# Where the ada rows of a macaron layer are summed: rates of the row queue, and an earlier stage for one vector

## The chip, the cores and the metric

The kernel runs on one core of one Trainium2 chip. A core has TensorE (matmuls; PE in the profile, PEld its weight loads), VectorE (DVE), ScalarE (ACT), GpSimd (POOL) and SyncE (SP, which here only issues transfers), and 16 DMA engines that bring data from HBM to on-chip memory. The metric is device time in microseconds, the median of several executions; lower is better.

## The reference

One layer on 256 tokens of width 2048, in fp32: a half-weighted SwiGLU feed-forward, a token mixer of eight attention heads and four mLSTM heads, and a second feed-forward, each between an adaptive modulation and a gated residual with a layer norm.

```python
ada = (silu(c) @ w_ada + b_ada)                      # [1, 9*2048], w_ada is 2048 x 18432
sh1, sc1, g1, sh2, sc2, g2, sh3, sc3, g3 = split(ada, 9)
h = swiglu(ln(x) * (1 + sc1) + sh1, ffn1_w_in, ffn1_w_out)
x = ln(ALPHA * x + 0.5 * (1 + g1) * h, ln1_g, ln1_b)
h = mixer(ln(x) * (1 + sc2) + sh2, ...)              # w_in, heads, w_out
x = ln(ALPHA * x + (1 + g2) * h, ln2_g, ln2_b)
h = swiglu(ln(x) * (1 + sc3) + sh3, ffn2_w_in, ffn2_w_out)
x = ln(ALPHA * x + 0.5 * (1 + g3) * h, ln3_g, ln3_b)
```

The nine vectors of `ada` are numbered 0 to 8 in the kernel: 0, 3 and 6 are shifts, 1, 4 and 7 scales, 2, 5 and 8 gates. Each needs 2048 x 2048 weights, read once for a single row of `c`. The inner width of the feed-forwards is 5632.

## The kernel before, in words

**Matmuls.** All large products are done in three parts with split operands (`mm3`, lines 419 to 421): an operand is cast to a shortened format on ScalarE (`hi`, line 155) and the remainder is taken on VectorE (`lo`, line 156). Weights come in by `load_w`: a raw tile of 1 MB (three buffers, SyncE issues the transfer, line 382), then two splits of 128 x 1024 into `hi` and `lo` (six buffers each). A raw buffer is free again when both of its `lo` have been taken. Unless told otherwise one such load is 24 matmuls of 512 columns, or 48 of 256.

**Stages.** First feed-forward's input columns (`first_in`, then `ffn_in`), its output projection (`out_proj` with the tag `f1`), a hand-ordered `boundary` (residual, layer norm, modulation), the mixer's projections with the heads woven between (`cols_1024`, `cols_form_b`, `form_a_four`; `step` is called once per load), the mixer's output projection (`out_proj`, tag `mx`), a second boundary, and the second feed-forward in the same manner (tag `f2`).

**The output projection.** `out_proj` goes through the 2048 output columns in three passes, of widths 1024, 512 and 512. In the first pass the hidden rows are also split (`h_rows`). For the first feed-forward a pass is 22, 11 and 11 loads. The additions into the residual (`add_up`, which multiplies by `gate`) of one pass are put into the list `late` and carried out a few steps at a time (`catch_up`) during the next pass. `lastg` is true in the last pass. In that pass the last four loads have no pump; for `f1` they call `ada.end_step()` instead. `finish1` first calls `need(6)` and then sets `ada.owed` to 0.

**The ada rows.** VectorE sums the products of `w_ada` with `silu(c)`: for each of 16 blocks of 128 rows, a transfer of 128 x 1024 numbers (512 KB, into `araw`, two buffers, line 189) and one operation `acc = raw * csil + acc` (line 170). Such a step is called a row here. Sixteen rows make a unit: half a gate (1024 columns; two units per gate), or a pair, 512 columns each of a shift and of its scale (four units per pair of vectors). A unit ends with a tail of five steps (`pair_tail`, `gate_tail`): splits, a sum over the partitions by TensorE (`bc`, line 183), and for pairs a product with the identity and a reduction (lines 200 to 204).

The class `AdaQueue` holds the units in a fixed order: gate 2, pairs 3 (four units), `pair(6, 0)`, `pair(6, 1)`, gate 5, `pair(6, 2)`, `pair(6, 3)`, gate 8. `pump(rate)` is called once per weight load: it does one step of a waiting tail, adds the rate to `owed`, and issues rows while `owed` is at least 1. Two things hold a unit back: its `stage`, when the queue's `stage` is still lower, and the accumulator. A unit without a place of its own uses the one tile `acc`, and waits until no tail of another such unit is open; the credit goes on growing meanwhile. `pair(6, 1)` is summed in the lower half of the tile `gate`, which the first feed-forward's residual reads in the first pass of its projection; the second half of gate 5 is summed in the upper half, which the second and third passes read. `need(n)` runs rows and tails until n units are done.

The rates are `R_F` and `R_IN` for the first feed-forward's input columns, `R_OUT` for its output projection, `R_MX` for the mixer up to its output projection, and `R_A`, `R_B` for the second feed-forward.

**Order on the engines.** Each engine executes its instructions in a fixed order. A planner makes that order ahead of the run, from the program's order, the buffers and its own estimates; `pinned()` keeps a row behind the latest weight split and the latest use of hidden rows, and the boundaries are ordered by hand.

Of the kernel before, what the change touches and what calls it, by code (L numbers as in the profile page):

```python
# [32 lines left out]
def layer_kernel(  # L33
# [35 lines left out]
    def mm_tile(name, four=False):  # L69
        turn[0] = 0 if four else turn[0] % 5 + 1  # L70
        if turn[0] == 5:
            return fifth_tile(name)
        return pm.tile([P, 512], F32, tag="mm", bufs=4, name=name)
# [205 lines left out]
    ada = AdaQueue()  # L279
# [98 lines left out]
    def load_w(src, nk, w, name, by_parts=False, behind=None, into=None):  # L378
        raw = wp.tile([P, nk, w], F32, tag="raw", bufs=3, name=f"raw_{name}")
        src = src.rearrange("(k p) n -> p k n", p=P)  # L380
        if not by_parts:
            SP.dma_start(raw, src)
        h = nk // 2 if nk * w <= 2048 else nk // 4
        for q in range(nk // h):
            if by_parts:
                SP.dma_start(raw[:, q * h:(q + 1) * h], src[:, q * h:(q + 1) * h])
            if into:
                hi, los = into[q]
                S.copy(hi, raw[:, q * h:(q + 1) * h, :])
                n = h // len(los)  # L390
                for i, lo in enumerate(los):
                    pin["w"] = V.tensor_tensor(out=lo, in0=raw[:, q * h + i * n:q * h + (i + 1) * n, :],
                                               in1=hi[:, i * n:(i + 1) * n, :].bitcast(F32), op=ALU.subtract).ins
                for kk in range(h):
                    yield q * h + kk, hi[:, kk, :], los[kk // n][:, kk % n, :]
                continue
            hi = wp.tile([P, h, w], F32R, tag="hi", bufs=6, name=f"hi_{name}{q}")
            lo = wp.tile([P, h, w], F32R, tag="lo", bufs=6, name=f"lo_{name}{q}")
            with ExitStack() as s:
                if behind:  # L400
                    s.enter_context(tc.issue_after(behind))
                pin["w"] = split(raw[:, q * h:(q + 1) * h, :], hi, lo).ins
            for kk in range(h):
                yield q * h + kk, hi[:, kk, :], lo[:, kk, :]
# [46 lines left out]
    def out_proj(w, rows, nk, tag, npump, finish, before=None, turned=False, spare=None, fine=None):  # L451
# [3 lines left out]
        late = []  # L455


        def catch_up(n):
            while n and late:
                if next(late[0], 0) == 0:  # L460
                    late.pop(0)
                else:
                    n -= 1
        for width in (1024, 512, 512):
# [4 lines left out]
                us = us[nu // 2:] + us[nu // 4:nu // 2] + us[:nu // 4]  # L469
            ps = {(a, b): mm_tile(f"o_{tag}{col}{a}{b}") for b in range(nb) for a in range(2)}  # L470
            lastg = col + width == D
            held = []

            def products(a, args, last=us[-1] * kn + kn - 1):
                ts_ = slice(a * P, (a + 1) * P)
                for k, hh, hl, hi, lo in args:
                    for b in range(nb):
                        mm3(ps[a, b], hh[:, ts_], hl[:, ts_], hi[:, b * 512:(b + 1) * 512],
                            lo[:, b * 512:(b + 1) * 512], k == us[0] * kn, k == last)
# [25 lines left out]
            def add_up(a, ps=ps, col=col, bs=range(nb), stats=True):  # L505
                for b in bs:
                    cs = slice(col + b * 512, col + (b + 1) * 512)
                    r = res[:, a, cs]
                    o = unwoven(ps[a, b])
                    V.tensor_tensor(out=o, in0=o, in1=halves(gate[:, cs]), op=ALU.mult)  # L510
                    yield
                    V.scalar_tensor_tensor(out=halves(r), in0=halves(r), scalar=ALPHA, in1=o,
                                           op0=ALU.mult, op1=ALU.add)
                    yield
                    if a and stats:
                        add_stats(cs)
                    elif stats:
                        V.bn_stats(st[0][:, col // 512 + b, :], r)
                    yield

            for i, u in enumerate(us):
                hs = []
                if before:
                    before(u * kn)
                into = spare() if spare and lastg and i == nu - nheld else None
                for k in range(u * kn, u * kn + kn, 2):
                    hs += rows(k)
                for kk, hi, lo in load_w(w[u * kn * P:(u + 1) * kn * P, col:col + width], kn, width,
                                         f"{tag}o{col}_{u}", into=into):
                    arg = (u * kn + kk, *hs[kk], hi, lo)  # L530
                    if lastg and i >= nu - nheld or not lastg and i == nu - 1:
                        held.append(arg)
                    else:
                        for a in range(2):
                            if a and lastg and fine is not None:
                                products(a, [arg], nk - nheld * kn - 1)
                            else:
                                products(a, [arg])
                if not lastg and i == nu - 1:

                    late += [add_up(a, bs=(b,)) for b in range(nb) for a in range(2)]
                    products(0, held)
                    catch_up(2)
                    products(1, held)
                else:
                    catch_up(2)
                if not lastg or i < nu - 4:
                    npump()
                elif tag == "f1":
                    ada.end_step()  # L550
# [209 lines left out]
    def entry_of(load, got, u0, u1):  # L760
        for u in range(u0, u1):
            got[u] = []
            for item in load(u):
                got[u].append(item)
                yield

    R_F, R_IN, R_OUT, R_MX, R_A, R_B = 1.25, 1.2, 1, 1.42, 1.05, .6
    NP = 2  # L770
    right = dict(side="right")
    def at(rate):
# [223 lines left out]
    low, high = (lambda: gate[:, :1024]), (lambda: gate[:, 1024:])  # L996
# [2 lines left out]
        ada.pair(3, j)  # L999
    ada.pair(6, 0)  # L1000
    ada.pair(6, 1, low, stage=1)
    ada.gate(5, 1.0, None, high, stage=1)
    ada.pair(6, 2)
    ada.pair(6, 3, low, stage=2)
    ada.gate(8, 0.5, high, None, stage=2)
    for j in range(4):
        fa = first_ada(j + 1) if j < 3 else load_mixer_smalls()
        for i in range(NS):
# [79 lines left out]

    hi_places("1")
    out_proj(ffn1_w_out[0], h_rows, KF, "f1", at(R_OUT), finish1, spare=lambda: dead_rows(ln1_g, ln1_b, "1"))  # L1090
    xp, npool = ent["xp"], ent["np"]
    xT = new_xT("mx")
    raws = [mo_raw(u) for u in range(3)]
    mow = {}
    fence, _, xs, ws = boundary(*ent["f"], ent["lgb"], 3, "1", xT, entry_of(mo_load, mow, 3, 6), KD, raws)
    ada.stage = 1
    lnp.release()
    ent["pools"].pop().release()

# [11 lines left out]
    mx = tc.alloc_tile_pool(name="mx", bufs=1, **right)  # L1111
# [401 lines left out]
    def before(k):  # L1513
        until([f"row{i}" for i in (k, k + 1)])
        if k == 2:
            need(10)
# [42 lines left out]
    def dead_heads():  # L1559
        hi = mx.tile([P, 2, 2, 512], F32R, tag="yF", name="yw")  # L1560
        lo = [mx.tile([P, 1, 512], F32R, tag="qk", bufs=4, name=f"yw{k}") for k in range(4)]
        return [(hi[:, q], lo[2 * q:2 * q + 2]) for q in range(2)]

    out_proj(w_out[0], y_rows, KD, "mx", step, finish2, before, True, dead_heads)
    xp, npool = ent["xp"], ent["np"]
    xT = new_xT("f2")
    raws = [gu_raw(u) for u in range(3)]
    guw = {}
    fence, mr2, xs, ws = boundary(*ent["f"], lgb, 6, "2", xT, entry_of(gu_load, guw, 3, 4), 8, raws)
    ada.stage = 2  # L1570
    lnp.release()


# [76 lines left out]
    def finish3(products, add_up, st):  # L1650
        to_out(products, add_up, st, ent["lgb"])

    out_proj(ffn2_w_out[0], h_rows, KF, "f2", at(R_B), finish3, spare=lambda: dead_rows(ln3_g, ln3_b, "3"),
             fine=fine)
    ent["dead"].release()
# [32 lines left out]
```

## Time and profile before

| | us |
|---|---|
| median of three executions | 1882.77 |
| lowest and highest | 1878.36, 1888.13 |
| the profiled execution | 1878.17 |
| its span, first to last instruction | 1876.2 |
| TensorE busy | 1838.5 (98%) |
| VectorE busy | 1429.2 (76%) |
| ScalarE busy | 900.5 (48%) |

The stages, from the span's start: input columns of the first feed-forward to 525, its output projection 525 to 756, boundary 756 to 794, the mixer's projections and heads 794 to about 1050, its output projection to about 1150, boundary to about 1176, the second feed-forward to the end. The granted TensorE clock was 0.996 of full speed over the span. An engine's idle time matters here only where TensorE waits for it.

### The profile page before, as it was taken

To read this page: it belongs to the slowest core of one execution; us is meant where nothing else is said; L and a number is where in the kernel's file an instruction comes from. 1 tells how busy PE (TensorE), PEld (TensorE's weight loads), DVE (VectorE), ACT (ScalarE), POOL (GpSimd) and SP (SyncE) were. 2 spreads that over 40 slices of the span, in tenths; PEclk is the share of its full clock that TensorE was granted. 3 is DMA by queue.
4 is the path that set the end of the run, shared out by engine and by line. 5 is a ranking of instruction groups with operands and counts; after the bars stand their busy time and mean duration, and the time that the engine had idled before them with its cause. 6 is when DMAs were issued, how large, how long until landed. Compare 5 with 4: busy or idle time off the path is not lost.

```text
span 1876.2 us, 32153 instructions
## 1 busy us (share of the span) xinstructions
PE 1838.5 (98%) x13161; PEld 1719.4 (92%) x13161; DVE 1429.2 (76%) x1771; ACT 900.5 (48%) x1272; POOL 62.2 (3%) x92
## 2 busy tenths in 40 slices
PE   7999999999999999999989999999999999999997
PEld 5999999999998888699989887999999999988887
DVE  6889989778788886878889888868876665564655
ACT  3554453434463433845566645565444444454441
POOL 1211200000000000100000000000000000000000
PEclk9999999999999999999999999999999999999999
DMA  9979968999898897499879893988778766566663
GB/s 365 383 267 320 325 228 277 322 330 331 275 321 293 310 324 289 142 307 329 297 265 323 311 322 131 343 291 271 253 251 265 260 223 195 191 204 203 205 204 146
DMA packets 283915, 510.90 MB, mean 272 GB/s; under 512 B 10834, under 2 KB 134386, under 8 KB 282744
## 3 DMA queue, kind: packets, MB, share of 16 engines
q1 hardware_dynamic: 275656, 477.90, 75.0%
q0 software_dynamic: 8112, 30.95, 4.8%
q8 instruction: 103, 1.69, 0.4%
q14 instruction: 44, 0.36, 0.1%
HBM read 506.71 MB, written 2.10 MB: 271 GB/s over the span
## 4 chain that ended last, share of the span: by engine, by line
PE 42%; DMA 7%; DVE 7%; issue 2%; ACT 1%; POOL 0%; DVEq 0%; ACTq 0%; POOLq 0%
DMA ar<-in_w_ada_dram 6%; PE gu_f L420 5%; PE gu_f L419 5%; PE gu_f L421 5%; PE o_f L420 4%; PE o_f L419 4%; PE o_f L421 4%; PE fh L419 2%; PE fh L420 2%; PE fh L421 2%; PE fs L420 2%; PE fs L421 2%; PE fs L419 1%; DVE acc L170 1%; PE ge L747 1%
## 5 line engine op out<-in xcount | busy, mean ns | idle before, releaser
L170 DVE SCALAR_TENSOR_TENSOR acc<-ar,csil,acc 128x1024 f32<-128x1024 f32 (+1 forms) x167 | 211.9, 1270 | 73.0 <-DMA ar<-in_w_ada_dram 72.1
L419 PE MATMUL s<-xhi_f,hi_s 128*128 128x256 f32 x768 | 212.9, 278 | 1.1 <-DVE hT L969 0.9
L421 PE MATMUL s<-xhi_f,lo_s 128*128 128x256 f32 x768 | 212.4, 277 | 0.8 <-DVE lo_s L156 0.7
L420 PE MATMUL s<-xlo_f,hi_s 128*128 128x256 f32 x768 | 212.5, 277 | 0.0
L421 PE MATMUL gu_f<-xhi_f,lo_f2i 128*128 128x256 f32 x768 | 211.6, 275 | 0.0
L420 PE MATMUL gu_f<-xlo_f,hi_f2i 128*128 128x256 f32 x768 | 211.5, 275 | 0.0
L419 PE MATMUL gu_f<-xhi_f,hi_f2i 128*128 128x256 f32 x768 | 211.5, 275 | 0.0
L156 DVE TENSOR_TENSOR lo_f2i<-raw_f2i,hi_f2i 128x1024 fp32r<-128x1024 f32 x96 | 117.6, 1225 | 90.2 <-ACT hi_f2i L155 89.9
L421 PE MATMUL gu_f<-xhi_f,lo_f1i 128*128 128x256 f32 x640 | 176.5, 276 | 0.8 <-DVE lo_f1i L156 0.8
L420 PE MATMUL gu_f<-xlo_f,hi_f1i 128*128 128x256 f32 x640 | 176.3, 275 | 0.0
L419 PE MATMUL gu_f<-xhi_f,hi_f1i 128*128 128x256 f32 x640 | 176.3, 275 | 0.0
L156 DVE TENSOR_TENSOR lo_f2o<-raw_f2o,hi_f2o 128x1024 fp32r<-128x1024 f32 x86 | 105.2, 1225 | 89.3 <-ACT hi_f2o L155 89.3
L155 ACT CAST hi_f2i<-raw_f2i 128x1024 fp32r<-128x1024 f32 x96 | 100.5, 1047 | 131.8 <-PE gu_f L420 120.6
L155 ACT CAST hi_s<-raw_s 128x1024 fp32r<-128x1024 f32 x96 | 99.8, 1052 | 128.9 <-PE s L420 86.7
L419 PEld LDWEIGHTS s<-xhi_f,hi_s 128*128 128x128 f32 x768 | 148.2, 193 | 1.4 <-DVE hT L969 1.1
L421 PEld LDWEIGHTS s<-xhi_f,lo_s 128*128 128x128 f32 x768 | 148.3, 193 | 1.2 <-DVE lo_s L156 1.2
L420 PEld LDWEIGHTS s<-xlo_f,hi_s 128*128 128x128 f32 x768 | 148.5, 193 | 0.4 <-DVE xlo_f L339 0.4
L420 PEld LDWEIGHTS gu_f<-xlo_f,hi_f2i 128*128 128x128 f32 x768 | 147.6, 192 | 0.2
L419 PEld LDWEIGHTS gu_f<-xhi_f,hi_f2i 128*128 128x128 f32 x768 | 147.6, 192 | 0.2
L421 PEld LDWEIGHTS gu_f<-xhi_f,lo_f2i 128*128 128x128 f32 x768 | 147.7, 192 | 0.0
L155 ACT CAST hi_f2o<-raw_f2o 128x1024 fp32r<-128x1024 f32 x86 | 90.1, 1048 | 119.5 <-PE o_f L421 111.2
L155 ACT CAST hi_f1o<-raw_f1o 128x1024 fp32r<-128x1024 f32 x86 | 88.7, 1047 | 112.9 <-PE o_f L421 48.6
(450 smaller groups left out, 5456.0 us busy)
## 6 DMA issues: line engine op xcount, KB each, us to landing
ar<-in_w_ada_dram SPq DMA_DIRECT2D x230, 512.0 KB, 5.5
raw_f2i<-in_ffn_w_in_dram SPq DMA_DIRECT2D x48, 1024.0 KB, 5.2
raw_s<-in_ffn_w_in_dram SPq DMA_DIRECT2D x47, 1024.0 KB, 7.8
raw_f1o<-in_ffn_w_out_dram SPq DMA_DIRECT2D x44, 1024.0 KB, 7.2
raw_f2o<-in_ffn_w_out_dram SPq DMA_DIRECT2D x44, 1024.0 KB, 5.1
raw_f1i<-in_ffn_w_in_dram SPq DMA_DIRECT2D x40, 1024.0 KB, 7.7
ar<-in_w_ada_dram POOLq DMA_DIRECT2D x45, 512.0 KB, 6.8
raw_mxo<-in_w_out_dram SPq DMA_DIRECT2D x16, 1024.0 KB, 7.3
```

Of the source, the lines that this page charges most:

```text
L155: S.copy(hi, src)
L156: return V.tensor_tensor(out=lo, in0=src, in1=hi.bitcast(F32), op=ALU.subtract)
L170: V.scalar_tensor_tensor(out=acc, in0=raw, scalar=csil[:, k:k + 1], in1=acc, op0=ALU.mult, op1=ALU.add)
L419: PE.matmul(o, ah, bh, start=start, stop=False)
L420: PE.matmul(o, ah, bl, start=False, stop=False)
L421: PE.matmul(o, al, bh, start=False, stop=stop)
L747: PE.matmul(unwoven(ps[a, b]), xs[a, k], halves(raws[u][:, q, b * 512:(b + 1) * 512]), start=k == 4 * a, stop=False)
```

## The change

`R_OUT` goes from 1 to 1.4 and `R_MX` from 1.42 to 1.15. The stages of the queue get one more number: `pair(6, 1, low)`, the sixth vector's second part, stays at stage 1, and stage 1 now begins in the last column pass of the first output projection instead of after the first boundary. The first boundary sets stage 2 and the second stage 3, and the units that were bound to them are renumbered. An assertion says that in both feed-forwards no addition of an earlier pass is left over when a pass ends.

```diff
@@ out_proj
             lastg = col + width == D
+            if lastg and tag == "f1":
+                ada.stage = 1
             held = []
...
                 if not lastg and i == nu - 1:
-
+                    assert tag == "mx" or not late
                     late += [add_up(a, bs=(b,)) for b in range(nb) for a in range(2)]
...
-    R_F, R_IN, R_OUT, R_MX, R_A, R_B = 1.25, 1.2, 1, 1.42, 1.05, .6
+    R_F, R_IN, R_OUT, R_MX, R_A, R_B = 1.25, 1.2, 1.4, 1.15, 1.05, .6
...
     ada.pair(6, 0)
     ada.pair(6, 1, low, stage=1)
-    ada.gate(5, 1.0, None, high, stage=1)
+    ada.gate(5, 1.0, None, high, stage=2)
     ada.pair(6, 2)
-    ada.pair(6, 3, low, stage=2)
-    ada.gate(8, 0.5, high, None, stage=2)
+    ada.pair(6, 3, low, stage=3)
+    ada.gate(8, 0.5, high, None, stage=3)
...
     fence, _, xs, ws = boundary(*ent["f"], ent["lgb"], 3, "1", xT, entry_of(mo_load, mow, 3, 6), KD, raws)
-    ada.stage = 1
+    ada.stage = 2
...
     fence, mr2, xs, ws = boundary(*ent["f"], lgb, 6, "2", xT, entry_of(gu_load, guw, 3, 4), 8, raws)
-    ada.stage = 2
+    ada.stage = 3
```

## The prediction

> **What bounds the kernel now.** I read the page first, then the busy time by stage, then TensorE's own waits, and last the rows of the ada sums and the stock of split weights in the first output projection.
>
> ```profile
> span 1876.2 us, 32153 instructions
> PE 1838.5 (98%) x13161; PEld 1719.4 (92%) x13161; DVE 1429.2 (76%) x1771; ACT 900.5 (48%) x1272; POOL 62.2 (3%) x92
> L170 DVE SCALAR_TENSOR_TENSOR acc<-ar,csil,acc 128x1024 f32<-128x1024 f32 (+1 forms) x167 | 211.9, 1270 | 73.0 <-DMA ar<-in_w_ada_dram 72.1
> ar<-in_w_ada_dram SPq DMA_DIRECT2D x230, 512.0 KB, 5.5
> ```
>
> TensorE is busy 98% of the span, so a change that leaves its instructions alone, as this one does, can win at most where it waits. One ada row costs 1.27 us of VectorE and a transfer of 512 KB, and VectorE, which works in order, stood idle 72.1 us for those transfers.
>
> ```profile
> 15.00:60.00 45.00, 42.97 (x289) 34.46 (x289) 33.81 (x53) 20.98 (x31) 4.83 (x7) 1.00 1.04 383
> ...
> 300.00:525.00 225.00, 224.21 (x1993) 223.32 (x1992) 177.64 (x182) 95.52 (x114) 1.08 (x2) 1.00 0.95 312
> 525.00:640.00 115.00, 115.00 (x536) 100.88 (x535) 96.86 (x98) 55.93 (x67) 0.00 (x0) 1.00 0.92 316
> 640.00:700.00 60.00, 60.00 (x279) 52.61 (x278) 52.64 (x55) 24.27 (x25) 0.00 (x0) 1.00 0.87 298
> 700.00:756.00 56.00, 56.00 (x260) 48.55 (x258) 39.01 (x57) 22.48 (x29) 2.68 (x4) 1.00 0.72 266
> ...
> 794.00:950.00 156.00, 150.70 (x1143) 144.15 (x1143) 130.74 (x182) 83.72 (x142) 3.44 (x8) 1.00 0.92 310
> 950.00:1110.00 160.00, 156.21 (x1046) 145.43 (x1045) 136.03 (x210) 92.45 (x185) 3.78 (x3) 0.99 0.88 307
> ```
>
> The columns are the window, its length, then PE, PEld, DVE, ACT and POOL busy, the granted clock, the DMA engines' share and GB/s. The first output projection is 525 to 756: TensorE never idles there. The mixer's projections are 794 to 1110: TensorE idles 5.3 + 3.8 = 9.1 us. The waits of TensorE in the mixer, in full:
>
> ```profile
> PE pr_fb L421 <- DVE lo_fb L156: 3.2, 1, 3.2
> PE sps L1400 <- DVE dm L1406: 2.4, 1, 2.4
> PE o_mx L421 <- DVE ylo L156: 1.4, 1, 1.4
> PE b_mv L420 <- DVE lo_mv L156: 1.1, 1, 1.1
> PE bc L183 <- DVE alo L156: 0.4, 1, 0.4
> PE o_mx L419 <- DVE res L512: 0.4, 1, 0.4
> PE pr_m L421 <- DVE lo_m L156: 0.4, 1, 0.4
> PE b_fv L420 <- DVE lo_fv L156: 0.3, 1, 0.3
> ```
>
> All are waits for VectorE, 9.6 us in sum (the window reaches a little past 1110), and 5.0 us of them (pr_fb, b_mv, pr_m, b_fv) are for the low half of a weight, which stands behind ada rows on VectorE. That is all that a lighter mixer can give back.
>
> **The change part by part.** *How many rows move.* Each pump adds its rate to a credit and spends whole rows. By the queue's own rules 59 of its rows lie ahead of the projection in both versions. In the projection 40 pumps are called (22, 11, and 7 of the last pass). Before, at 1.0, the sixth unit's rows end in the fifth pump of the last pass and the next unit must wait for its tail, so 37 rows are taken and 3.25 of credit are dropped where `finish1` clears it: 96 in all. After, at 1.4, there are 56 of credit. The three units of `pair(3,..)` end in the eighth pump of the second pass, `pair(6,0)` runs to the fifth pump of the last pass, and `pair(6,1)`, open since the start of that pass, gets 3 rows: 115. So 19 rows and one pair's tail move from mixer to projection. In the mixer 57 pumps at 1.42 gave 80 rows, to row 176, where the stage stops them; at 1.15 they are 61, to the same row.
>
> ```profile
> 525.00:640.00 115.00, 0.00 (x0) 0.00 (x0) 30.25 (x24) 0.00 (x0) 1.00 0.92 316
> 640.00:700.00 60.00, 0.00 (x0) 0.00 (x0) 17.43 (x14) 0.00 (x0) 1.00 0.87 298
> 700.00:756.00 56.00, 0.00 (x0) 0.00 (x0) 2.55 (x2) 0.00 (x0) 1.00 0.72 266
> ...
> 794.00:950.00 156.00, 0.00 (x0) 0.00 (x0) 49.73 (x40) 0.00 (x0) 1.00 0.92 310
> 950.00:1110.00 160.00, 0.00 (x0) 0.00 (x0) 45.94 (x37) 0.00 (x0) 0.99 0.88 307
> ...
> 572.00:614.00 42.00, 0.00 (x0) 0.00 (x0) 14.87 (x12) 0.00 (x0) 1.00 0.90 301
> ...
> 654.00:700.00 46.00, 0.00 (x0) 0.00 (x0) 17.43 (x14) 0.00 (x0) 1.00 0.93 317
> ```
>
> These are the ada rows alone (the DVE column, with their count) by window: 40 run in the projection before (three that the planner had carried over from the stage ahead), 77 in the mixer's windows. After I expect 59 and 58.
>
> *What the projection pays.* VectorE is busy 96.9 + 52.6 + 39.0 = 188.5 of 231 us there. 19 rows add 24.1 us and the tail six operations like the one below, 4.1 us: 216.7 us, 94%. The DMA engines move 115 x 316 + 60 x 298 + 56 x 266 = 69.1 MB; 19 rows add 10.0: 79.1 MB, 342 GB/s over 231 us, under the 383 that the window 15 to 60 shows. On averages both fit, with little to spare. But rows come in bursts: while a pair's tail takes five pumps no row is issued, and the credit then comes at once, 5 rows before, 7 or 8 after. What a burst does is seen in these rows: of the groups, of SyncE's issues, of the waits of SyncE (525 to 756) and of VectorE (525 to 640, then 640 to 700), and the operations on `lo_f1o` from 500 on.
>
> ```profile
> L200 DVE TENSOR_TENSOR dg<-bc,ident 128x512 f32<-128x512 f32 x2 | 1.4, 692 | 1.3 <-PE bc L183 1.3
> ...
> 576.80 0.37 SPq L382 DMA_DIRECT2D raw_f1o<-in_ffn_w_out_dram  x1
> 579.64 2.70 SPq L189 DMA_DIRECT2D ar<-in_w_ada_dram  x2
> ...
> 603.95 0.46 SPq L382 DMA_DIRECT2D raw_f1o<-in_ffn_w_out_dram  x1
> ...
> SPq L382 <- DVE lo_f1o L156: 71.1, 29, 5.9
> ...
> DVE acc L170 <- DMA ar<-in_w_ada_dram: 11.8, 10, 2.2
> ...
> DVE acc L170 <- DMA ar<-in_w_ada_dram: 7.0, 7, 2.1
> ...
> 500.00:571.20 71.20, 26.67 (x71) 13.46 (x71) 26.43 (x22) 1.00 0.88 296
> 500.00:612.75 112.75, 50.85 (x134) 25.40 (x134) 42.16 (x36) 1.00 0.89 299
> 500.00:640.00 140.00, 66.78 (x176) 33.37 (x177) 57.50 (x48) 1.00 0.91 311
> 500.00:654.60 154.60, 75.09 (x198) 37.52 (x198) 64.80 (x54) 1.00 0.89 304
> 500.00:700.00 200.00, 101.32 (x267) 50.74 (x268) 83.97 (x70) 1.00 0.90 307
> ```
>
> Two rows go between one weight load and the next, no more, since `araw` has two buffers. The five weight loads from 576.80 to 603.95 are 6.8 us apart. TensorE uses a load up in 5.2 us: each fills two split buffers, and 176 matmuls on `lo_f1o` (the row to 640.00), four to a buffer, fill 525 to 640, 115/44 = 2.6 us a buffer. The loop is: SyncE waits for a raw buffer until VectorE has split it, and VectorE waits for the row's transfer (11.8 us in the first pass, 7.0 in 640 to 700). So the stock of split buffers falls. It is, in the last rows of the fence, the DVE count less a quarter of the PE count (at 612.75 one split had only begun, so one less): 4.25 buffers at 571, 1.5 at 613, 4.0 at 640, 4.5 at 655, 3.25 at 700. In the first pass 12 rows cost 2.75 buffers, 7.1 us: 0.6 us a row. In the second, where the hidden rows need no more splitting, 14 rows cost 1.25, 3.3 us: 0.23 a row. With few rows (613 to 640) the stock regains 2.5 buffers, 6.5 us in 27, or 1.25 us per load used.
>
> After, the bursts follow one another. Start at about 10 us of stock. `pair(3,2)`: 16 rows in the first pass, -9.6, so 0.4 left; three loads without rows, +3.7. `pair(3,3)`: five rows at 0.6 and eleven at 0.23, -5.5: TensorE stands about 1.5 us. Three and a half loads, +4.4; then 19 rows of the sixth vector at 0.23, -4.4. The ends of the first and third burst touch zero, and I put 1 us on each: **+3.5 us** for the projection. Bounds: 0, since 300 to 525 ran at 1.2 rows a pump with 0.8 us idle; and with all rows at 0.6, 0 + 5.9 + 7.0 = **13 us**.
>
> [...]
>
> *What the mixer gains.* Of its waits I take the four for low weights and `bc`, **-5.4 us**: up to 950 there would be about 33 rows for 40, 9 us of VectorE. Bounds: nothing, and -9.6, all eight. `sps` waits for a head's mask product and `ylo` for a head's rows; they hang on the attention chain more than on rows.
>
> *What else moves.* With 1.15 `pair(6,2)` ends three pumps before the boundary, so 4.55 rows of credit gather behind its tail and are spent in one pump after it, 5 rows where before there was 1.
>
> ```profile
> 1176.00:1200.00 24.00, 23.72 (x192) 22.94 (x191) 20.00 (x21) 14.96 (x21) 0.00 (x0) 1.00 1.02 328
> ```
>
> The DMA engines are full there and the stock is just being laid up. Four more rows at 0.23 are **+1 us**; bounds 0 and 4 x 1.27 = 5. SyncE's queue carries the 19 transfers at 0.4 us each ahead of weight loads, which is in the price per row; POOL's moves no one's work past another's. The renumbered stages and the assertion cost nothing: they issue nothing, and first-pass additions that read the low half of the gate are over before the last pass, so the sixth vector's sum waits for none of them. If they were not, its first row would hold VectorE, at the price of the 13 us bound.
>
> **Sum.** -5.4 + 3.5 + 1 = -0.9 us, on a profiled execution of 1878.2 (span 1876.2): 1877.3. The median of the runs shown, 1882.8, stands 4.6 above that execution, which gives 1881.9 there. I say 1881, nearer the median, as it is of three runs. About 0.5%, 9.4 us, is what a measurement of this kernel can tell from no change; three runs spread 9.8.
>
> **The rivals.** *A, slower: the projection starves.* Mechanism: VectorE in order, waiting for rows with two buffers. For it: 216.7 us of work plus the waits for rows, (11.8 + 7.0) x 59/40 = 27.7, are 244 us in a stage of 231, 13 too many, the same as all rows at 0.6. Against: the second pass showed 0.23, and VectorE has 17 us free in 700 to 756. Price: +14 with the first stall, so -5.4 + 14 + 1 = +9.6, 1887.8, or 1892.4 by the median. It decides when the second and third bursts cost more than 0.6 a row.
>
> *B, the projection hides all:* as in 300 to 525. Then 0 there, and all eight waits gone: -9.6, 1868.6, or 1873 by the median. Against: the stock of 1.5 at 613 with a rate of 1.0.
>
> *C, the mixer keeps its waits:* the change moves rows but the waits belong to new weight streams and heads. 0 + 3.5 + 1: 1882.7, or 1887. For it: the longest two stand at a switch of weights and in a head. That the sixth vector's part does not begin early falls in here too: then three rows stay in the mixer and nothing else alters.
>
> **How the numbers follow.** Forecast 0.5, A 0.15, B 0.15, C 0.2. Faster by over 0.5%: B's better half, 0.09. Slower: A and the edge of C, 0.18. Between them 0.73. The range takes in C, most of A and the nearer half of B: 1872 to 1893; the forecast's own is 1876 to 1886.
>
> **What would show it.** 59 rows in the projection's windows, 58 in the mixer's; VectorE about 94% busy and the DMA engines near 340 GB/s between 525 and 756; a stock under one buffer at the end of the first two bursts, and TensorE idle there 2 to 5 us for `lo_f1o` where it idled 0; `pr_fb`, `b_mv`, `pr_m` and `b_fv` waiting under 1 us in sum; five rows between the boundary and 1195. The prediction is wrong if TensorE idles over 8 us in the projection, or if the mixer's idle time stays at 9.

## The result: slower by 1.15%, and the profile after

| | before | after |
|---|---|---|
| median of the runs shown | 1883.68 us (4 runs) | 1903.77 us (4 runs) |
| lowest and highest | 1878.36, 1888.13 | 1897.41, 1907.56 |
| ratio, 95% interval | | 1.0115 (1.0075 to 1.0154) |
| profiled execution, its span | 1878.17, 1876.2 | 1902.89, 1901.2 |

The forecast was no change, 1881 within 1872 to 1893. In the functions below `out_proj`'s new lines the changed kernel's line numbers are two higher: `add_up` multiplies by the gate at L512 (L510 before) and adds at L514 (L512). The page of the changed kernel:

```profile
span 1901.2 us, 32158 instructions
PE 1842.7 (97%) x13161; PEld 1721.0 (91%) x13161; DVE 1430.7 (75%) x1771; ACT 900.2 (47%) x1272; POOL 61.5 (3%) x92
```

The work is the same, to a matmul; only waits can have come. Each boundary begins with transposes at L355, whose first start is a stage mark. Their group, of the kernel before and then of the changed one (minimum, median, maximum in ns, then first and last start):

```profile
L355 PE MATMUL tp<-ident,n x48: 272/273/330, 757.0 to 1168.7; 128*128 128x128 f32 x48
```

```profile
L355 PE MATMUL tp<-ident,n x48: 272/273/332, 788.8 to 1186.5; 128*128 128x128 f32 x48
```

The first boundary starts 31.8 us later. The same answer for the stretch around the second boundary puts its first transpose at 1152.8 and at 1170.6. So the three stages read:

| stage, profiled executions | before | after | difference | forecast |
|---|---|---|---|---|
| to the first boundary | 757.0 | 788.8 | +31.8 | +3.5 |
| first to second boundary (mixer) | 395.8 | 381.8 | -14.0 | -5.4 |
| second boundary to the end | 723.4 | 730.6 | +7.2 | +1 |
| sum | 1876.2 | 1901.2 | +25.0 | -0.9 |

The profiled execution of before, 1878.17, lies below all four of its runs and that of the changed kernel close to its median, so the stages add up to more than the 21.7 us of the ratio. How much one execution can differ shows in j_mx, a run further down: it alters the mixer's rate alone, its instructions come in the order of before on every engine up to 803 us, and yet its first boundary starts at 766.1, 9.1 us later. The +31.8 is uncertain by about as much.

All three signs were forecast, and all three sizes were too small, most of all the first. The rows of the sum came out as counted: the windows of the changed kernel, ada rows alone (the DVE column).

```profile
525.00:660.00 135.00, 0.00 (x0) 0.00 (x0) 39.83 (x32) 0.00 (x0) 0.97 0.88 302
660.00:725.00 65.00, 0.00 (x0) 0.00 (x0) 18.82 (x16) 0.00 (x0) 1.00 0.89 310
725.00:788.00 63.00, 0.00 (x0) 0.00 (x0) 14.84 (x12) 0.00 (x0) 0.89 0.84 292
```

60 with one cut by a window's edge, for 59 forecast. The averages were right as well: 302 GB/s over 263 us is 79.4 MB for 79.1 forecast, and VectorE's 215.0 us of work were put at 216.7. What those averages did not tell is what stands behind a late row. The waits of TensorE in the projection (engine and line waited for: us, times, longest):

```profile
PE bc L183 <- ACT ahi L155: 11.2, 2, 9.5
PE o_f L419 <- DVE res L514: 8.5, 1, 8.5
PE bc L183 <- DVE alo L156: 3.4, 3, 1.4
PE o_f L420 <- DVE lo_f1o L156: 1.4, 1, 1.4
```

Before, this stage had none but 0.6 us at its end. The last line is the only one that the prediction priced, the stock of split weights. It stood at 610.9, in the burst of `pair(3,2)`, for which 1 us was put down; in the bursts of `pair(3,3)` and of the sixth vector, for which 1.5 and 1 were, TensorE waited for no `lo`. The other 23.1 us stand elsewhere. First the hole for `res`, at the change from the first pass to the second. VectorE in order (start, duration, and in brackets the idle time ahead):

```profile
650.01 1.29 DVE L170 SCALAR_TENSOR_TENSOR acc<-ar,csil,acc 128x1024 f32<-128x1024 f32 x1 [0.74 <-DMA ar<-in_w_ada_dram]
651.21 1.22 DVE L156 TENSOR_TENSOR lo_f1o<-raw_f1o,hi_f1o 128x1024 fp32r<-128x1024 f32 x1
652.35 1.28 DVE L170 SCALAR_TENSOR_TENSOR acc<-ar,csil,acc 128x1024 f32<-128x1024 f32 x1
653.54 1.22 DVE L156 TENSOR_TENSOR lo_f1o<-raw_f1o,hi_f1o 128x1024 fp32r<-128x1024 f32 x1
654.68 1.29 DVE L512 TENSOR_TENSOR o_f<-o_f,gate 128x512 f32<-128x512 f32 x2
655.88 0.68 DVE L514 SCALAR_TENSOR_TENSOR res<-res,o_f 128x512 f32<-128x512 f32 x1
```

The next pass's matmuls need an accumulator that the addition at 654.68 to 656.6 frees. It stands behind a burst of rows and splits, and TensorE stood from 648.2 to 656.7. Then the long hole near the end, first TensorE, then ScalarE and VectorE:

```profile
751.59 0.38 PE L421 MATMUL o_f<-hi_f1o,lo 128*128 128x512 f32 x1
761.51 0.79 PE L183 MATMUL bc<-ahi,trir 128*128 128x512 f32 x1 [9.54 <-ACT ahi L155]
763.72 0.80 PE L183 MATMUL bc<-alo,trir 128*128 128x512 f32 x1 [1.42 <-DVE alo L156]
764.32 0.63 PE L419 MATMUL o_f<-dhi,hi 128*128 128x512 f32 x1
...
755.70 1.99 ACT L155 CAST hi_f1o<-raw_f1o 128x1024 fp32r<-128x1024 f32 x2 [6.95 <-DMA raw_f1o<-in_ffn_w_out_dram]
760.84 0.62 ACT L155 CAST ahi<-acc 128x512 fp32r<-128x512 f32 x1 [3.15 <-DVE acc L170]
...
756.77 1.23 DVE L156 TENSOR_TENSOR lo_f1o<-raw_f1o,hi_f1o 128x1024 fp32r<-128x1024 f32 x1 [3.83 <-ACT hi_f1o L155]
759.52 1.28 DVE L170 SCALAR_TENSOR_TENSOR acc<-ar,csil,acc 128x1024 f32<-128x1024 f32 x1 [1.52 <-DMA ar<-in_w_ada_dram]
```

`bc`, the partition sum of `pair(6,0)`, stands in TensorE's own order, waits for ScalarE's `ahi`, that for the pair's last row, and that for a transfer issued at 749.75. Ahead of the row VectorE stood 3.83 us for a load of weights that was late too: it was issued at 745.52, and ScalarE got it at 755.70.

The same place shows what a late weight load does by itself. Here are TensorE's two longest waits in the projection of j_mx, where VectorE has no row from 715 on, and ScalarE there:

```profile
PE bc L183 <- ACT ahi L155: 5.1, 1, 5.1
PE o_f L419 <- DVE res L512: 1.9, 1, 1.9
```

```profile
741.01 1.99 ACT L155 CAST hi_f1o<-raw_f1o 128x1024 fp32r<-128x1024 f32 x2 [4.41 <-DMA raw_f1o<-in_ffn_w_out_dram]
742.91 0.61 ACT L155 CAST ahi<-acc 128x512 fp32r<-128x512 f32 x1
```

`ahi` stands in ScalarE's order behind the casts of a load that landed late. So part of this stage's holes can open without the change, and did not in the profiled execution of before. Finally the clock:

```profile
652.90:659.70 6.80, 3.00 (x7) 2.47 (x8) 6.37 (x8) 0.00 (x0) 0.00 (x0) 0.50 0.93 307
748.00:760.00 12.00, 3.97 (x19) 3.14 (x17) 6.52 (x8) 2.74 (x3) 0.18 (x1) 0.80 1.02 396
755.30:769.00 13.70, 6.07 (x14) 4.47 (x15) 9.45 (x10) 5.12 (x6) 0.00 (x0) 0.50 0.97 354
```

Around both long holes the granted clock is 0.50, and matmuls start 0.43 us apart (764.7 to 768.6) instead of 0.22 (746.6 to 751.6). TensorE was busy for 3.00 + 6.07 us of it, and by these spacings half of that would have done at the full clock: some 4.5 us more, an estimate. Holes 24.5 and half clock 4.5 make 29.0 of the 31.8; where the rest lies was not worked out. The middle row shows the DMA engines full, at a share of 1.02 and 396 GB/s, while the second hole forms: two rows, loads, and the layer norm's two 1 MB parameter transfers, which GpSimd issues at 747.1 and 747.7.

The mixer's two windows of the changed kernel, all instructions (PE is the first of the busy columns):

```profile
824.00:980.00 156.00, 156.00 (x1196) 150.28 (x1195) 131.27 (x190) 89.46 (x153) 2.84 (x8) 1.00 0.89 304
980.00:1127.00 147.00, 147.00 (x991) 137.34 (x990) 119.05 (x187) 88.17 (x177) 3.78 (x3) 1.00 0.84 290
```

TensorE idles nowhere in them: all waits shown before are gone. In the second feed-forward there are new ones (window 1190 to 1330; before, 0.3 us):

```profile
PE fh L419 <- ACT hi_fh L155: 1.9, 1, 1.9
PE gf L419 <- ACT hT L1617: 1.7, 1, 1.7
PE fh L421 <- DVE lo_fh L156: 0.8, 1, 0.8
PE fs L421 <- DVE lo_fs L156: 0.8, 1, 0.8
PE fh L419 <- ACT hT L1591: 0.5, 1, 0.5
```

### The profile page after: what moved, and what is told of

The parts are those of the page before. It is cut to its first block, busy times and chain, and to the rows that moved or that the text cites. A ratio compares the mean times of both kernels' runs of the same rounds, so it can differ in the third digit from the quotient of the medians.

```text
span 1901.2 us, 32158 instructions
## 1 busy us (share of the span) xinstructions
PE 1842.7 (97%) x13161; PEld 1721.0 (91%) x13161; DVE 1430.7 (75%) x1771; ACT 900.2 (47%) x1272; POOL 61.5 (3%) x92
## 4 chain that ended last, share of the span: by engine, by line
PE 52%; DMA 2%; DVE 2%; issue 1%; ACT 1%; POOL 0%; DVEq 0%; SPq 0%; ACTq 0%; POOLq 0%
PE gu_f L420 5%; PE gu_f L421 5%; PE gu_f L419 5%; PE o_f L421 4%; PE o_f L419 4%; PE o_f L420 4%; PE fs L421 2%; PE fs L419 2%; PE fs L420 1%; PE o_mx L421 1%; PE o_mx L420 1%; PE o_mx L419 1%; DMA raw_fh<-in_ffn_w_in_dram 1%; PE fh L421 1%; PE fh L419 1%
```

## Experiments

Theory: rows arrive late, because two row buffers and a landing of 5.1 us (the median of `ar` in the changed kernel, 525 to 788) bound their rate, VectorE stands in order in front of them, and whatever comes behind a late row stops TensorE. Rivals: a particular thing behind the row is the cause (the partition sums in TensorE's order, the credit's bursts, the sixth vector's early part, the parameter transfers); VectorE's work; or SyncE's order of issue. Each ratio is to the kernel before, run on the same chip. "Projection", "mixer" and "rest" are the three stages of the table above in each profiled execution, against 757.0, 395.8 and 723.4 before and 788.8, 381.8 and 730.6 after.

**The transfers or the VectorE work.** In x_dma the rows of this projection are summed from a constant; in x_dve the transfers stay and only an eighth of each row is summed.

```diff
 x_dma, in the first output projection
-            SP.dma_start(raw, src[k * P:(k + 1) * P])
-            ada_acc(acc, raw, k)
+            ada_acc(flat, ident.unsqueeze(1).to_broadcast([P, 8, P]), k)
 x_dve, in the first output projection
-            ada_acc(acc, raw, k)
+            ada_acc(acc[..., :64], raw[..., :64], k) if k else ada_acc(acc, raw, k)
```

> The changed kernel in which the ada rows pumped in the first output projection are summed from a constant on the chip instead of their weights: VectorE's operations are the same in number and size, the rows' transfers (56 x 512 KB) and the waits for them are left out there. Theory 1 (late transfers: VectorE stands in order behind a row that has not landed, and the additions, low halves and partition sums behind it make TensorE stand): the holes of the projection (24.6 us from 600 to 765) nearly all go, under 4 us left; with the half-speed stretches -25 to -32 us, 1872 to 1879. Theory 2 (VectorE's own work fills the stage): half of the holes or more stay, 1890 or more.

> The counterpart: the transfers of the rows in the first output projection stay, but VectorE sums 128 of their 1024 columns (the rest of those sums is left out). VectorE has about 56 x 1 us less to do there. Theory 1: the rows still land late and everything behind them waits, so half of the holes or more stay (12 us or more of 24.6), 1888 or more. Theory 2: the holes go, 1872 to 1880. If the projection is short of both, both runs gain about half.

x_dma: 1882.94 (10 runs), 1.0008 (0.9985 to 1.0032); projection 769.0, mixer 381.7, rest 731.6. x_dve: 1890.30 (10 runs), 1.0044 (1.0020 to 1.0068); projection 774.8, mixer 381.7, rest 731.4. TensorE's longest waits in the projection of x_dma, then of x_dve (their line numbers are shifted again):

```profile
PE bc L183 <- ACT ahi L155: 6.2, 1, 6.2
PE o_f L425 <- DVE lo_f1o L156: 1.1, 1, 1.1
```

```profile
PE o_f L422 <- DVE res L517: 3.3, 1, 3.3
PE bc L183 <- DVE alo L156: 3.0, 1, 3.0
PE bc L183 <- ACT ahi L155: 2.8, 1, 2.8
```

Without transfers 19.8 of the projection's 31.8 us go, with an eighth of the sums 14.0. They overlap (33.8 together), so the loss is the two in one loop: a row that comes late and 1.27 us of VectorE behind it. The `res` hole needs both: it is 8.5 us in the changed kernel, 3.3 in x_dve and 0.2 in x_dma. x_dma fell between its two theories, with 7.5 us of holes where under 4 or over half were expected. Its 6.2 us are the hole of j_mx again: `ahi` behind casts of a load that kept ScalarE waiting 7.23 us, from 736.8 to 744.0, with the DMA engines at 0.99 and the parameter transfers issued at 733.8 and 734.3. Its whole time is level with before.

**One more row buffer.** Three `araw`, paid for with one split buffer (five `lo` for six), on the changed kernel with the credit cleared (h_clear, below) and on the kernel before.

```diff
-tag="araw", bufs=2   ...   tag="lo", bufs=6
+tag="araw", bufs=3   ...   tag="lo", bufs=5
```

> The changed kernel with three row buffers instead of two, five low-half buffers instead of six, and the credit cleared behind the second boundary as in h_clear. Theory of the two-buffer loop: VectorE's waits for rows in the projection (22.8 us) fall by half or more, and so do TensorE's holes there (24.6 us), in spite of the shorter stock: 1870 to 1886. Theory of work (VectorE and the DMA engines are full on average): the holes stay at 18 or more, with one low buffer fewer perhaps more, 1895 or more.

> The kernel before with three row buffers and five low-half buffers. By the two-buffer theory the mixer's waits of 9.6 us fall by half or more, -4 to -12 us, unless the shorter stock gives it back; by the theory of work the shorter stock costs 2 to 10 us.

a3lo5: 1911.84 (4 runs), 1.0160 (1.0099 to 1.0221). b3lo5: 1891.24 (10 runs), 1.0038 (1.0011 to 1.0066). VectorE's waits in 525 to 788, of h_clear and of a3lo5:

```profile
DVE acc L170 <- DMA ar<-in_w_ada_dram: 27.1, 22, 4.3
```

```profile
DVE lo_f1o L156 <- ACT hi_f1o L155: 23.5, 12, 4.6
DVE acc L170 <- DMA ar<-in_w_ada_dram: 8.2, 6, 2.0
DVE lo_f1o L156 <- PE o_f L420: 7.9, 4, 4.6
```

The waits for rows fall from 27.1 to 8.2 us, and TensorE's own in the projection from 22.2 to 11.5 (`res` 5.3, `lo_f1o` 3.4, `bc` 1.6, `hi` 1.2). In b3lo5 the mixer's waits outside the boundaries fall from 9.6 to 0.4. So with two buffers rows keep VectorE waiting, and a third takes most of that away. That this would bring the time down is not shown: 1911.84 is far from the 1870 to 1886 that the loop was expected to give. The split buffer that paid for it is the likely reason: there is a wait of 5.6 us for `n` at each boundary, where it was 0.6 to 0.9, and VectorE waits 7.9 us for a free `lo`. Neither version gains, and the two effects were not separated.

**SyncE's order.** The projection's rows issued by GpSimd (pool_q), and all rows in the changed kernel with cleared credit (a_pool) and in the kernel before (b_pool).

```diff
-            SP.dma_start(raw, src[k * P:(k + 1) * P])
+            G_.dma_start(raw, src[k * P:(k + 1) * P])
```

> The changed kernel with the rows' transfers of the first output projection issued by GpSimd instead of SyncE; bytes, buffers and VectorE's work are the same. If SyncE's order makes rows and weights late (each waits behind the other's buffer), the holes of the projection fall from 24.6 to under 10 us and the time to 1880 to 1892. If the DMA engines are full or two row buffers are too few, the holes stay at 18 or more and the time at 1895 or more.

> The changed kernel with all rows of the queue issued by GpSimd in every stage, and the credit cleared behind the second boundary (5 to 7 us in h_clear). By the order theory 1872 to 1886, perhaps faster than before; by the theory of full engines 1890 or more.

> The kernel before with all rows of the queue issued by GpSimd. By the order theory the mixer's waits (9.6 us) fall by half or more and its time by 4 to 10 us; by the theory of full engines no change within 4 us. GpSimd's own issue could make it slower where its gate loads and layer norm loads stand behind a row that waits for a buffer.

pool_q 1926.48 (4 runs), 1.0223 (1.0184 to 1.0263); a_pool 1925.64 (4), 1.0219 (1.0176 to 1.0262); b_pool 1927.96 (4), 1.0226 (1.0177 to 1.0274). The waits of TensorE in pool_q, 525 to 800, and its wait of VectorE for rows to 788:

```profile
PE o_f L419 <- DVE res L514: 13.8, 1, 13.8
PE o_f L420 <- DVE lo_f1o L156: 13.1, 8, 3.7
PE bc L183 <- ACT ahi L155: 8.1, 2, 7.5
...
DVE acc L170 <- DMA ar<-in_w_ada_dram: 45.5, 34, 3.4
```

Freed from SyncE's order the rows are later still, 45.5 us for 22.8, and now the stock of splits runs out too. The gain expected of another order did not come, and no expectation had a loss of this size. Full engines on average do not explain it: their share fell to 0.79 over the stage, from 0.88. But the edit changes more than the order: GpSimd's issue takes 0.72 us a row in pool_q, where SyncE's takes 0.37 in the changed kernel, and the profile lists these transfers under another queue, `software_dynamic`. So these runs do not show what part SyncE's order has. Nothing is gained in any of the three. The kernel before loses as much when its rows take this way, mostly in the mixer (422.9 us for 395.8): with slow rows, the place where they are summed decides only which stage pays.

**One thing behind the row at a time.** a_hold lets no tail step of the sixth vector into the last pass; c_defer only adds credit and takes a tail step in the last three loads of the first pass, so that no row is issued there; lnp_cut sets the first layer norm's gain and offset to one instead of loading them; no_last pumps no rows in the last pass; cnh is c_defer, no_last and the cleared credit together.

```diff
 a_hold
-            if self.tails:
+            if self.tails and not self.hold:      # hold from the last pass until after need(6)
 c_defer, in the first pass of f1
-                    npump()
+                    ada.owed += R_OUT; ada.end_step()      # for i >= nu - 3
 lnp_cut
-        queue.dma_start(lg, ...); queue.dma_start(lb, ...)
+        G_.memset(lg, 1.0); G_.memset(lb, 1.0)      # for the first layer norm
 no_last
-                if not lastg or i < nu - 4:
+                if not lastg or i < nu - 4 and tag != "f1":
```

> The changed kernel with one thing altered: in the last column pass of the first output projection no tail step of an ada unit is taken, so the two partition sums (bc) of the sixth vector's first part no longer stand in TensorE's queue there; the rows stay as they are. Theory 1 (fixed order: TensorE stands because bc is queued ahead of the products and waits for the row chain): the hole of 9.5 + 1.4 us at 752 to 764 and the half-speed stretch after it (7.5 us at half speed, 3.7 us lost) go, about -14 us from 1903.8, so 1886 to 1893. Theory 2 (more rows than VectorE and the DMA engines can carry there): TensorE waits for lo_f1o instead in the same place, 1899 or more.

> The changed kernel with one thing altered: in the last three loads of the first column pass the pump only adds credit and takes a tail step, so the burst of 7 rows falls behind the first addition into the residual. Theory 1 (order: the addition that frees the accumulator for the second pass stands behind rows on VectorE): the hole of 8.5 us at 648 and the half speed after it (1.5 us) go, about -10 us, 1890 to 1897. Theory 2 (work): the rows are the same in number, TensorE waits as long a little later, 1900 or more.

> The changed kernel without the two 1 MB transfers of the first layer norm's gain and offset (both are set to one by GpSimd; the loading of these two vectors is left out). Keeping the partition sums out of the last pass gave back little (a_hold), so theory 1 is now that the hole at 752 to 764 is a jam of transfers: the parameters, two rows and a weight load, with the DMA engines full from 748 to 760. Then without 2 MB (about 5 us at the 405 GB/s measured there) the hole of 9.5 + 1.4 us falls to 3 to 6 and the time by 6 to 10 us. Theory 2 (VectorE has too much to do, whatever the transfers): the hole stays within 2 us and so does the time.

> The changed kernel with no ada row pumped in the last column pass of the first output projection (9 of the 16 rows of the sixth vector's first part are taken in the second pass, the other 7 and the second part's 3 go to the mixer). Theory 1 (the jam of transfers in the last four loads): the hole at 752 to 764 goes with its half-speed stretch, -13 to -15 us, and ten more rows in the mixer cost it back 2 to 5: net -8 to -13 from the changed kernel. Theory 2 (a lack of VectorE time over the whole projection): the holes at 623 to 657 are as before (they lie ahead), and the last one keeps half or more; net -5 or less.

> The changed kernel with three places mended together: credit only (no rows) in the last three loads of the first column pass, no rows in the last pass, credit cleared behind the second boundary. If each hole belongs to its place, 8.5 us at 648, 11 at 752 to 764 and 5 in the second feed-forward go with their half-speed stretches, and ten rows in the mixer cost 3: about -22, 1878 to 1885, level with before. If the waiting only moves on to the next thing behind the rows (as in a_hold and c_defer), 1890 or more.

| | us (runs) | ratio, 95% | projection, mixer, rest |
|---|---|---|---|
| a_hold | 1901.70 (4) | 1.0123 (1.0084 to 1.0162) | 784.1, 383.6, 731.9 |
| c_defer | 1902.47 (4) | 1.0128 (1.0094 to 1.0161) | 785.4, 382.7, 731.3 |
| lnp_cut | 1899.89 (4) | 1.0102 (1.0063 to 1.0142) | 781.1, 381.8, 734.3 |
| no_last | 1897.22 (10) | 1.0078 (1.0055 to 1.0101) | 781.7, 384.4, 730.8 |
| cnh | 1890.57 (10) | 1.0051 (1.0028 to 1.0074) | 764.1, 385.3, 732.0 |

TensorE's longest waits in the projection of a_hold, of c_defer and of no_last:

```profile
PE o_f L419 <- DVE res L514: 7.5, 1, 7.5
PE o_f L420 <- DVE lo_f1o L156: 6.7, 4, 5.5
```

```profile
PE bc L183 <- ACT ahi L155: 14.1, 3, 8.8
PE tp L355 <- DVE n L349: 3.0, 1, 3.0
```

```profile
PE o_f L419 <- DVE res L514: 8.5, 1, 8.5
```

Each edit removes or shortens the wait that it aims at, and the time hardly falls: the intervals of all four overlap that of the changed kernel. With the partition sums out of the last pass, TensorE waits there 5.5 us for weights instead: `bc` in its order is not by itself what makes that hole. With the first pass's rows deferred the `res` hole is gone, and a `bc` of 3.5 at 693 and 3.0 at the boundary have come. Without the parameter transfers the last hole shrinks from 9.5 + 1.4 to 3.3 + 2.2, as expected of a jam of transfers, and the boundary starts 7.7 us earlier. That is less than the same instructions differ from one execution to the next, and the whole gains 4 us by the medians where 6 to 10 were expected, which the intervals do not tell from nothing. Without rows in the last pass its hole goes, but the rows come back as `bc` 5.4 at 1291. Only the three together bring the projection near its old length, at 764.1, with rows left for later; the whole is still 0.5% slower, not level with before. That profiled execution was cnh's shortest, 1883.3 of 1883.3 to 1898.0.

**The other terms.** h_clear drops the credit behind the second boundary; e_stage undoes the second half of the change; r12 and i_in are other rates; j_mx is the kernel before with only the mixer's rate altered.

```diff
 h_clear, behind the second boundary
+    ada.owed = 0
 e_stage
-    ada.pair(6, 1, low, stage=1)
+    ada.pair(6, 1, low, stage=2)
 r12: R_OUT, R_MX = 1.2, 1.28     i_in: R_IN, R_OUT, R_MX = 1.45, 1.0, 1.2     j_mx: R_MX = 1.3 (R_OUT 1)
```

> The changed kernel with the queue's credit set to 0 behind the second boundary, so that one row is issued in the first pump of the second feed-forward and not five. If the burst of rows is what costs there, TensorE's idle time between 1195 and 1330 falls from 5.7 to about 1 us and the stretch of half clock at 1230 goes: -5 to -7 us, 1896 to 1899. If it is the boundary or the weight transfers themselves, nothing alters (1902 to 1906).

> The changed kernel with the second half of the change undone: the sixth vector's second part is held until the first boundary, so 3 rows fewer run in the last pass. If those 3 rows matter in the jam (they are 1.5 MB, 4 us at the measured rate), the hole at 752 to 764 falls by 2 to 5 us. If the first part's rows and its tail are what is late, the hole stays at 9 to 11 and the time within 3 us of the changed kernel.

> The changed kernel with half of the change in rates: 1.2 in the output projection and 1.28 in the mixer. If the loss grows evenly with the rows in the projection, half of it, 1890 to 1895. If it depends on whether bursts fall on the change of a pass and on the last loads, it may lie anywhere from 1878 to 1905; the holes then stand where a burst meets them.

> The changed kernel with other rates: 1.45 in the input columns (instead of 1.2), 1.0 in the output projection, 1.2 in the mixer: five more rows go into the input columns, where the stock of split weights was long, no partition sum of the sixth vector stands in the last pass, and the mixer is as light as in the change. Theory 1: the mixer keeps its gain of 10 to 14 us, the input columns pay 0 to 2, the projection 0 to 4: 1871 to 1880, faster than before (1883.7). Theory 2 (the first feed-forward cannot carry more rows at all): TensorE waits for lo_f1i or lo_f1o by as much as the mixer wins, 1884 or more.

> The kernel before with the mixer's rate alone lowered from 1.42 to 1.3 (173 rows at the second boundary instead of 176; the pair of the last three goes to the second feed-forward). The changed kernel's mixer stages were 14 us shorter. If a row in the mixer has an even price, 14 us for 19 rows, the seven fewer rows by its output projection are worth 3 to 5 us, and 1 or 2 are paid back after the boundary. If it is the places where bursts meet a switch of weights, the time moves either way by up to 4 us. Nothing over 5 us slower is expected by either.

| | us (runs) | ratio, 95% | R_MX | projection, mixer, rest |
|---|---|---|---|---|
| h_clear | 1896.23 (4) | 1.0088 (1.0058 to 1.0117) | 1.15 | 787.3, 382.1, 724.7 |
| e_stage | 1896.94 (6) | 1.0085 (1.0057 to 1.0113) | 1.15 | 782.5, 383.3, 724.3 |
| i_in | 1895.24 (4) | 1.0087 (1.0057 to 1.0118) | 1.20 | 783.9, 385.0, 722.8 |
| r12 | 1893.67 (10) | 1.0056 (1.0035 to 1.0077) | 1.28 | 773.1, 391.2, 729.1 |
| j_mx | 1885.23 (10) | 1.0016 (0.9991 to 1.0042) | 1.30 | 766.1, 392.1, 735.8 |

- h_clear: the rest falls to 724.7, and the waits behind the boundary to 0.5 + 1.2 us. The credit's burst is 5.9 of the +7.2 in these executions, as was expected; the intervals of the whole times overlap.
- e_stage: without the early start the projection gives back 6.3 us, and the rest 6.3, since by the queue's rules the mixer's credit goes into the three rows more. That execution was the shortest of its six, 1891.77, and the interval overlaps that of the changed kernel, so a price of the early start is not shown. The rates alone still cost 0.85%.
- r12: half the step, half the loss.
- i_in: the rows moved a stage further up do not end free either. The input columns show holes of 1.2 to 3.1 us and a `res` hole of 7.9 stands at the pass change again, though the projection's rate is the old 1.0; another of 5.3 us, for the hidden rows that VectorE splits, stands at its start. A gain, the first theory, did not come; of the second, 1884 or more, the time came true, but most of the waiting is not for `lo`.
- j_mx: no difference that can be told. Its profiled execution was the longest of its ten; its 766.1 is what the instructions of before can take up to the boundary.
- The mixer's length, in single executions, follows its rate: 395.8 at 1.42, 392.1 at 1.30, 391.2 at 1.28, 385.0 at 1.20, 381.8 at 1.15.

## Why the prediction was wrong, by its steps

- **What the projection pays, +3.5: measured +31.8.** The step that failed. A row was priced by what it takes from the stock of split weights. That price was of the right order (1.4 us of stalls for 3.5, in the first burst alone), and it was the smallest part. VectorE's order also holds the addition that frees the next pass's accumulators (8.5 us), and the pairs' partition sums stand in TensorE's order (14.6 us), where the tail was counted as six VectorE operations and no matmul. Both are late when a row is late, however many weights are in stock; the partition sum is late too when a load of weights is, through ScalarE's order. The bound of 13 used the same price, so it did not bound these.
- **The half clock, left out.** At a granted clock of 0.50 around the two longest holes TensorE took some 4.5 us more, by the estimate above. The trace of before had the sign: its stretch 953.7 to 957.1, behind the 2.4 us for `sps`, was at 0.51.
- **"POOL's moves no one's work past another's"** speaks of order alone. GpSimd's two parameter transfers, issued at 747.1 and 747.7 and landing 8.6 and 11.3 us later, were under way together with rows and loads while the DMA engines' share was 1.02 (748 to 760): without them, in lnp_cut, the last hole was 5.5 us and not 10.9. A gain in the whole time is not shown.
- **Rival A named the place and the mechanism** (VectorE in order, two buffers, waits for rows). x_dma and x_dve bear out the waits for rows, and a3lo5 the part of the two buffers in them, though not in the time. Its price, +14, was the average work over the stage's length; the measured loss is more than twice that. Its sign against, VectorE's 17 free us in 700 to 756, was no cover: the addition at 654.68 stood in order behind rows, and VectorE's free time from 700 on came too late for it.
- **The mixer, -5.4 of at most -9.6: measured -14.0.** "That is all that a lighter mixer can give back" was wrong. All eight waits went: between the two boundaries' marks TensorE's idle time fell from 12.2 to 2.6 us, 9.7 less. The other 4.3 us are shorter busy time, of which the half clock behind `sps` (3.4 us at 0.51) is at most 1.7, an estimate; the rest was not explained. The rate is its likely cause, by the five lengths above.
- **The burst behind the second boundary, +1 of at most 5: measured +7.2**, of which h_clear took 5.9 back. It was priced as rows by themselves; they alternate with that stage's first loads, which TensorE then waited for.
- **Right:** the rows (59), VectorE's work, the DMA volume, the credit's behaviour, the sign of each term. The limit set in advance, over 8 us of idle time in the projection, was passed with 24.5.
- **Open:** how the projection's loss divides into transfers and VectorE work, since the two overlap; how much of the +31.8 is the difference between two executions; and why rows issued by GpSimd come later.

## What to carry to other kernels

Ask of moved work not only how much of the stage it fills but what stands behind it on its engine, and behind that on the next: accumulators to be freed (8.5 us) and small matmuls in TensorE's order (14.6 us) stopped it here sooner than the weight stream did (1.4 us). A stage without idle time in TensorE has a margin that no average shows; when one hole there is mended and the time stays, as here, look for the cause in what comes late and not in the thing that waited. Bursts of saved credit fall on the start of the next stage; here dropping the credit took 5.9 us off that stage. Before a stage of one execution is compared with a stage of another, ask how much two executions of the same instructions differ.

## What the runs showed of the hardware

- The granted clock was 0.50 or 0.51 in spells of 3.4 us (before, from 953.7), 6.8 and 13.7 us (after, from 652.9 and 755.3). In the last it was still 0.50 for 7.5 us after TensorE's return at 761.5, with a second wait of 1.42 us in them; from 769.0 to 772.0 it was 1.00.
- 512 KB rows issued by GpSimd instead of SyncE made both kernels over 2% slower (a_pool 1.0219, b_pool 1.0226), in pool_q (1.0223) with the DMA engines less full (0.79 for 0.88).
- The same kernel's executions spread by 6 to 20 us in ten runs (r12 1889.7 to 1896.1, j_mx 1875.5 to 1895.8), so one execution's stage lengths are good to several microseconds only: the same instructions took 757.0 us to the first boundary in one execution and 766.1 in another.
